# A two-layer encoder trunk on one core: the last stage's gate columns begin behind its first rows, the first group is gated at the end, and convolutions that read PSUM banks go first

## The chip, the cores and the metric

The kernel runs on one core of one Trainium2 chip. The metric is the device time of one execution, in microseconds (us). All arithmetic is float32; a product is made of three matmuls on operands that are split in a high and a low part (below).

## What is computed

The reference, cut to what matters here:

```
sc = silu(c)
for l in (0, 1):
    shift, scale, gate = split(sc @ ada_w[l] + ada_b[l])        # 2048 columns each
    h = rmsnorm(x, g_pre[l]) * (1 + scale) + shift
    if l == 0:                                                   # mLSTM, 8 heads
        proj = h @ a_w_in
        qk = silu(causal_conv(proj[:, :4096], conv_w, conv_b))   # 4 taps along the tokens
        y = mlstm(qk, v, gates) ... @ a_w_out
    else:                                                        # band attention, 16 heads
        k, v = modulate(rmsnorm(x, kv_g)) @ kv_w
        y = (attention(h @ w_q, k, v) * silu(h @ w_z)) @ b_w_out
    x = x + gate * rmsnorm(y, g_post[l])
```

x has 512 tokens of 2048 columns. The last product, `@ b_w_out`, is 512 x 2048 by 2048 x 2048; its result y is multiplied column by column with `gate * g_post` and token by token with the reciprocal root of its mean square.

## The kernel before

All weights stand in DRAM in the order in which they are used (`stream()`), in pieces of up to 128 x 1024 floats. `wpiece` (L188) loads the next piece on SP's queue (L200, tile `wr`), has ScalarE (ACT) round it to its high part (L182, `wh`) and VectorE (DVE) subtract for the low part (L183, `wl`); the two together are `split`. `mm3` then issues three matmuls for each product (L224): hi*hi, hi*lo, lo*hi. Raw pieces have two buffers and a third where a spare pool is named (every third piece), high and low parts have three each, so a piece is split when TensorE (PE) has ended the piece three before it.

The tile framework builds the program: it puts each instruction in its engine's queue in an order that a scheduler sets from program order, priorities (`tc.high_priority(AHEAD)` moves what is in it ahead) and its own estimate of when things are ready; `keep_in_program_order` pins instructions of one kind among themselves. Each engine then works its queue strictly in order, SP's DMA queue too: an instruction that waits holds all that stand behind it. A pool's memory may be reused by a later pool, tile by tile.

The adaLN columns are sums over `sc`: for a block of 128 columns (`mod` column i) two loads of 128 x 1024 floats (`ada_load`, L378) and two DVE reductions (`ada_sum`, L382; a reduction and a short accumulator read each) against a broadcast copy of `sc`. There are 128 blocks; most are done in the background of heads 0 to 3 of the first layer (`background(n)`), the last 16 (blocks 80 to 95, the second layer's gate) in the last stage.

Heads 2 and 3 of the first layer: for each of four 128-column blocks of q and k, `proj_a` (L242) makes a product in a PSUM bank of `psP` (five banks), and `conv` (L526) reads that bank four times: ACT for one tap (L529) and DVE for three (L531), then SiLU and a split. After each, `background(4)` adds four reductions. The value product `ps_v` follows and takes four banks of the same pool.

The last stage (from L1086) works in four groups g of 512 output columns. `proj_b` (L245) goes through the 2048 rows of `b_w_out` two blocks k0, k0 + 1 at a time, each step with one weight piece and, for group 0, one load of two attention output tiles (`y2_tile`, L1100: DRAM `y2c[i]` to `y2r`, then `split` into the stationary tiles `y2`; the first two go to the weight pool, the others share two buffers of the pool `op`). A step is 24 matmuls for four token blocks m; group 3 is done in two halves of two token blocks with 12 matmuls a step. The dictionary `at` names what is called ahead of step k0. `evac` (L784) reads a finished bank: DVE multiplies with the broadcast gate row `gb` (the tile `ssum`) into `yo`, ACT sums the squares. `finish(m)` multiplies with the reciprocal root, adds x and stores.

The gate itself: `gate_sums` sums the up to four pending loads and issues the next four; `gates_out` (L564) multiplies four blocks with `g_post`, turns them to a row with one PE transpose (`ps_gg`), copies it with ACT and writes it to DRAM (`ggd`); `gate_row` (L780) loads the 512 columns of a group back to all partitions. The order is written in `gate_steps`:

```
gate_steps = {
    0: {0: gate_sums, 4: gate_sums, 8: gate_sums, 10: lambda: (gate_part(0), gate_row(1, 0)), 12: gate_sums},
    1: {0: gate_sums, 2: lambda: gate_part(1), 4: gate_sums, 8: gate_sums, 10: lambda: gate_part(2), 12: gate_sums},
    2: {0: gate_sums, 4: lambda: gate_part(3)},
    3: {},
}
```

Of the kernel before, what the change touches and what calls it, by code (L numbers as in the profile page):

```python
# [9 lines left out]
F32 = mybir.dt.float32  # L10
F32R = mybir.dt.float32r
AF = mybir.ActivationFunctionType
ALU = mybir.AluOpType
AX = mybir.AxisListType

P = 128
D = 2048
S = 512
KT = D // P
# [13 lines left out]
AHEAD = 300  # L33
RAW_BUFS = 2

PAIRS = [(0, 1), (2, 3)]
# [9 lines left out]
HALF = 3  # L46
# [78 lines left out]
CW = KVG + 16  # L125
CBIAS = CW + 128
# [6 lines left out]
def hybrid_trunk(ctx, tc, xT, xN, c, adaT, cols, wst, wg, ext, kc, out):  # L133
    nc = tc.nc
# [8 lines left out]
    def pool(name, bufs=1, **kw):  # L143
        return tc.tile_pool(name=name, bufs=bufs, reuse_waits="tile", **kw)
# [7 lines left out]
    csc = dram.tile([1, D], F32, name="csc")  # L152
# [15 lines left out]
    ssum = const.tile([P, S], F32, name="ssum")  # L168
# [7 lines left out]
    def col(i):  # L176
        return cl[:, i : i + 1]
# [3 lines left out]
    def split(hi, lo, src):  # L181
        nc.scalar.copy(hi, src)  # L182
        nc.vector.tensor_tensor(lo, src, hi.bitcast(F32), op=ALU.subtract)  # L183
# [58 lines left out]
    def proj_a(mat, xs, ps, t0=0, t1=S):  # L242
        proj(mat, xs, [ps], 8, 0, len(xs), len(xs) - 1, t0, t1)
# [107 lines left out]
    def newp(name):  # L351
        return psP.tile([P, S], F32, tag="p", name=name)

    def newa(name):
        return psA.tile([P, S], F32, tag="a", name=name)
# [25 lines left out]
    def ada_sum(i, j, at, pin=lambda ins: ins, sc=None):  # L381
        pin(nc.vector.tensor_tensor_reduce(  # L382
            at, at, (sc or scB)[:, j * D // 2 : (j + 1) * D // 2], 1.0, mod[:, i : i + 1] if j else col(CB + i),
            ALU.mult, ALU.add, mod[:, i : i + 1]
        ))
# [25 lines left out]
    for i in range(4):  # L411
        ps = newp(f"ps_c{i}")
# [9 lines left out]
    for q in range(4):  # L422
        pair = []
# [30 lines left out]
    for k0, k1 in BLOCKS:  # L454
# [10 lines left out]
        for i, acc in enumerate(later):  # L465
            ps = newa(f"ps_l{i}_{k0}")
# [56 lines left out]
            nc.tensor.transpose(pt[:, j * 8 : j * 8 + 8], e[:, j * P : (j + 1) * P], ident[:8, :8])  # L523
        nc.vector.tensor_copy(aT.rearrange("p a b -> p (a b)"), pt[:, :32])

    def conv(ps, ch, name):  # L526

        acc = tp.tile([P, S], F32, tag="t", name=f"cv_{name}")
        nc.scalar.activation(acc, ps, AF.Identity, bias=col(CBIAS + ch), scale=col(CW + 96 + ch))  # L529
        for d in range(1, 4):  # L530
            nc.vector.scalar_tensor_tensor(  # L531
                acc[:, d:], ps[:, : S - d], col(CW + 32 * (3 - d) + ch), acc[:, d:], op0=ALU.mult, op1=ALU.add
            )
        nc.scalar.activation(acc, acc, AF.Silu)
        t = hp.tile([P, 2, S], F32R, tag="qk", name=f"qk_{name}", bufs=4)
        split(t[:, 0, :], t[:, 1, :], acc)
        return t
# [12 lines left out]
    def background(n):  # L550

        for a in loaded:
            ada_sum(*a, tc.keep_in_program_order)
        loaded.clear()
        for b, (i, j) in enumerate(pending[:n]):
            p, bufs = (ap_, ADA_BUFS) if b < ADA_BUFS else (bp, 2)
            loaded.append(ada_load(i, j, p, bufs, tc.keep_in_program_order))
        del pending[:n]
# [28 lines left out]
    def pair(c, name, f=HEAD_PAIRS, at={}):  # L587
        z1, z2 = (acp.tile([P, 2, 256], F32, tag="so", name=f"{name}_{i}", bufs=6) for i in range(2))
        proj_s("a_w_in", h1, h1s, f, z1, z2, name, hq, (2, 2), at)
        return [z.rearrange("p a t -> p (a t)") for z in (z1, z2)]  # L590
# [32 lines left out]
    for h in range(NH):  # L623
        for i in (2 * h, 2 * h + 1):
            nc.sync.dma_start(bsc[i], ext[i].partition_broadcast(P))
        chs = [2 * h, 2 * h + 1, 16 + 2 * h, 16 + 2 * h + 1]
        if h == 0:
            so = oz[:4]
        qk = []
        for i in range(4):  # L630
            if h > HALF:
                if i % 2 == 0:
                    zs = pair((i // 2) * (V0 // 2) + h * DK, f"zq{h}_{i}")
                ps = zs[i % 2]
            elif h < 2:
                ps = (lead, qk1)[h][i]
            else:
                ps = newp(f"ps_qk{h}_{i}")
                proj_a("a_w_in", h1, ps)
            qk.append(conv(ps, chs[i], f"{h}_{i}"))  # L640
            if 1 < h <= HALF:
                background(4)
        zs = ps = None
# [45 lines left out]
        for i in range(4):  # L689
            if h >= HALF:  # L690
                f = HEAD_PAIRS if h > HALF else RAMP[i]
# [5 lines left out]
            elif h:  # L697
                ps = newp(f"ps_o{h}_{i}")
# [4 lines left out]
        for i in range(4):  # L703
            if h >= HALF:
                break
            if h:
                ps = newp(f"ps_z{h}_{i}")
                proj_a("a_w_in", h1, ps)
            else:
                ps = oz[4 + i]  # L710
# [12 lines left out]
        for i in range(4):  # L723
            d = slice(i * P, (i + 1) * P)
            ps = newa(f"ps_n{h}_{i}")
# [9 lines left out]
        ps = newa(f"ps_q{h}")  # L735
# [41 lines left out]

    gb = ssum

    def gate_row(layer, g):  # L780

        nc.sync.dma_start(gb, ggd[layer, 4 * g : 4 * g + 4, :].rearrange("k p -> (k p)").partition_broadcast(P))

    def evac(ps, m, g, dst):  # L784
        nc.vector.tensor_tensor(dst, ps, gb, op=ALU.mult)
        nc.scalar.activation(newa(f"sqy{m}_{g}"), ps, AF.Square, accum_out=ssq[:, 4 * m + g : 4 * m + g + 1])

    def row_rstd(m):
# [178 lines left out]
    bias = at.tile([P, S], F32, name="bias")  # L967
# [119 lines left out]
    op = ost.enter_context(pool("op", bufs=KT))  # L1087
    rp = ost.enter_context(pool("x2", bufs=8))
    yo = [[] for _ in range(4)]
# [26 lines left out]
            nc.sync.dma_start(out[m, :, g * S : (g + 1) * S], y)  # L1116

    scC = op.tile([P, D], F32, tag="sc", name="scC", bufs=1)
    nc.sync.dma_start(scC, csc.rearrange("a d -> (a d)").partition_broadcast(P))
    gate_cols = [(80 + i, j) for i in range(KT) for j in range(2)]  # L1120
    gate_in = []

    def gate_sums():

        for a in gate_in:
            ada_sum(*a, tc.keep_in_program_order, scC)
        gate_in[:] = [ada_load(i, j, op, 4, tc.keep_in_program_order) for i, j in gate_cols[:4]]
        del gate_cols[:4]

    def gate_part(g):  # L1130
        gates_out(1, 4 * g, 4 * g + 4, op, bufs=1)

    gate_steps = {
        0: {0: gate_sums, 4: gate_sums, 8: gate_sums, 10: lambda: (gate_part(0), gate_row(1, 0)), 12: gate_sums},
        1: {0: gate_sums, 2: lambda: gate_part(1), 4: gate_sums, 8: gate_sums, 10: lambda: gate_part(2), 12: gate_sums},
        2: {0: gate_sums, 4: lambda: gate_part(3)},
        3: {},
    }
    for g in range(4):
        if g:  # L1140
            spare[0] = op
        for pair in [range(4)] if g < 3 else PAIRS:
            ps = [newp(f"ps_y1_{g}_{m}") for m in pair]
            at = {4: lambda: finish(0), 6: lambda: finish(1)} if pair == PAIRS[1] else {}
            if 0 < g < 3:
                at = {k: lambda k=k: fetch_x(2 * (g - 1) + k // 12) for k in (2, 12)}
            add_at(at, gate_steps[g] if pair != PAIRS[1] else {})
            if g and pair != PAIRS[1]:
                add_at(at, {8: lambda: gate_row(1, g)})
            proj_b("b_w_out", y2_tile, ps, ms=pair, at=at, late=3 if pair == PAIRS[1] else 0)  # L1150
            with tc.high_priority(AHEAD):
                for p, m in zip(ps, pair):
                    yo[m].append(op.tile([P, S], F32, tag="o", name=f"yo{m}_{g}"))
                    evac(p, m, g, yo[m][g])
    finish(2)
    finish(3)
    assert wpos[0] == len(order)
# [56 lines left out]
```

## Time and profile before

| what | value |
|---|---|
| runs, us | 2832.49, 2839.56, 2838.55; median 2838.55 |
| profiled execution | 2837.93 us, of which the span from first to last instruction 2836.2 us |
| mean granted TensorE clock | 0.993 |
| PE busy | 2773.2 us, 98% of the span |
| DVE busy | 2153.3 us, 76% |
| ACT busy | 1372.7 us, 48% |
| last stage, first matmul to end of span | 2614.2 to 2836.2 us |

How to read it: the rows are of one execution. In a timeline row stand the start, the length, the engine, the line, the operation, output and input tiles, and in brackets how long the engine had been idle and what ended that. In a row of the stretches stand the limits, the length, the busy time of each engine with its count of instructions, the granted TensorE clock (1.00 is full speed) and the DMA engines' busy share. SPq is SP's DMA queue.

### The profile page before, as it was taken

To read this page: it belongs to the slowest core of one execution; us is meant where nothing else is said; L and a number is where in the kernel's file an instruction comes from. 1 tells how busy PE (TensorE), PEld (TensorE's weight loads), DVE (VectorE), ACT (ScalarE), POOL (GpSimd) and SP (SyncE) were. 2 spreads that over 40 slices of the span, in tenths; PEclk is the share of its full clock that TensorE was granted. 3 is DMA by queue.
4 is the path that set the end of the run, shared out by engine and by line. 5 is a ranking of instruction groups with operands and counts; after the bars stand their busy time and mean duration, and the time that the engine had idled before them with its cause. 6 is when DMAs were issued, how large, how long until landed. Compare 5 with 4: busy or idle time off the path is not lost.

```text
span 2836.2 us, 42097 instructions
## 1 busy us (share of the span) xinstructions
PE 2773.2 (98%) x15959; PEld 2443.3 (86%) x15959; DVE 2153.3 (76%) x3750; ACT 1372.7 (48%) x2034; POOL 0.2 (0%) x4
## 2 busy tenths in 40 slices
PE   7999999999999999999999999999999999999698
PEld 5787887888998989989898888888998999999587
DVE  7986988889885876858767445568875888988565
ACT  4234534233554554545545445568434566666223
POOL 0000000000000000000000000000000000000000
PEclk9999999999999999999999999999999999999899
DMA  8875797886232332323324657788435444444864
GB/s 293 301 253 176 248 333 263 309 304 247 94 116 90 105 112 86 109 99 103 118 90 162 214 198 235 235 279 279 147 134 197 145 130 127 122 130 138 292 234 170
DMA packets 177813, 526.02 MB, mean 185 GB/s; under 512 B 19093, under 2 KB 37557, under 8 KB 176969
## 3 DMA queue, kind: packets, MB, share of 16 engines
q1 hardware_dynamic: 177610, 523.33, 54.4%
q8 instruction: 125, 2.05, 0.3%
q14 instruction: 78, 0.64, 0.1%
HBM read 489.65 MB, written 38.85 MB: 186 GB/s over the span
## 4 chain that ended last, share of the span: by engine, by line
PE 78%; DVE 9%; DMA 8%; issue 3%; ACT 2%; SPq 0%; DVEq 0%; ACTq 0%
PE ps_y L224 18%; PE ps_v L224 9%; PE ps_azo L224 5%; DMA ada<-in_adaT 4%; PE ps_kv L224 4%; PE ps_az L224 3%; PE ps_bzo L224 3%; PE ps_cz L224 3%; PE ps_dz L224 3%; PE ps_czo L224 3%; PE ps_dzo L224 3%; PE ps_o L224 3%; DVE wl L183 3%; DVE ada L382 2%; DMA wr<-in_wst 2%
## 5 line engine op out<-in xcount | busy, mean ns | idle before, releaser
L182 ACT CAST wh<-wr 128x1024 fp32r<-128x1024 f32 (+3 forms) x586 | 585.7, 1001 | 718.7 <-PE ps_y L224 217.9
L183 DVE TENSOR_TENSOR wl<-wr,wh 128x1024 fp32r<-128x1024 f32 (+3 forms) x586 | 678.4, 1159 | 322.1 <-ACT wh L182 321.1
L224 PE MATMUL ps_y<-wh,y 128*128 128x512 f32 x1536 | 478.7, 392 | 24.1 <-ACT y L182 23.0
L224 PEld LDWEIGHTS ps_y<-wh,y 128*128 128x128 f32 x1536 | 289.4, 189 | 85.2 <-ACT y L182 23.8
L182 ACT CAST wsh<-ws 128x384 fp32r<-128x384 f32 (+1 forms) x261 | 163.3, 626 | 370.0 <-issue 139.1
L224 PE MATMUL ps_v<-wh,h 128*128 128x512 f32 x1024 | 324.6, 393 | 3.5 <-DVE cv L531 3.4
L224 PE MATMUL ps_y<-wl,y 128*128 128x512 f32 x768 | 300.2, 391 | 0.8 <-DVE wl L183 0.8
L183 DVE TENSOR_TENSOR wsl<-ws,wsh 128x384 fp32r<-128x384 f32 (+1 forms) x261 | 181.3, 695 | 120.2 <-ACT wsh L182 118.4
L224 PEld LDWEIGHTS ps_v<-wh,h 128*128 128x128 f32 x1024 | 193.7, 189 | 44.8 <-DVE cv L531 4.2
L224 PE MATMUL ps_v<-wl,h 128*128 128x512 f32 x512 | 200.6, 392 | 0.0
L224 PEld LDWEIGHTS ps_y<-wl,y 128*128 128x128 f32 x768 | 144.9, 189 | 31.3 <-DVE wl L183 1.5
L224 PE MATMUL ps_kv<-wh,hkv 128*128 128x512 f32 x512 | 159.2, 390 | 0.0
L382 DVE CUSTOM_DVE_ANT_0 ada<-ada,scB,cl 128x1024 f32<-128x1024 f32 x112 | 143.2, 1280 | 18.8 <-DMA ada<-in_adaT 18.3
L382 DVE CUSTOM_DVE_ANT_0 ada<-ada,scB,mod 128x1024 f32<-128x1024 f32 x112 | 143.3, 1280 | 17.5 <-DMA ada<-in_adaT 15.7
L207 DVE TENSOR_TENSOR ws<-wr 128x256 f32<-128x256 f32 (+1 forms) x261 | 131.6, 514 | 30.7 <-DMA wr<-in_wst 28.8
L224 PEld LDWEIGHTS ps_v<-wl,h 128*128 128x128 f32 x512 | 96.9, 189 | 19.8 <-issue 0.9
L224 PEld LDWEIGHTS ps_kv<-wh,hkv 128*128 128x128 f32 x512 | 96.1, 188 | 19.7
L224 PE MATMUL ps_azo<-h,wh 128*128 128x256 f32 (+1 forms) x406 | 101.4, 331 | 1.2 <-DVE zo L318 1.2
L224 PE MATMUL ps_l<-h,wh 128*128 128x512 f32 x320 | 99.4, 392 | 0.8 <-ACT oz L469 0.8
L224 PE MATMUL ps_kv<-wl,hkv 128*128 128x512 f32 x256 | 99.8, 390 | 0.3 <-DVE wl L183 0.3
L224 PE MATMUL ps_czo<-h1s,wsh 128*128 128x256 f32 x468 | 89.3, 283 | 0.0
L209 DVE TENSOR_TENSOR ws<-wr 128x128 f32<-128x128 f32 (+1 forms) x261 | 84.7, 334 | 3.4
(383 smaller groups left out, 6214.6 us busy)
## 6 DMA issues: line engine op xcount, KB each, us to landing
wr<-in_wst SPq DMA_DIRECT2D x520, 512.0 KB, 3.9
ada<-in_adaT SPq DMA_DIRECT2D x256, 512.0 KB, 6.7
xt<-nsc SPq DMA_DIRECT2D x48, 256.0 KB, 2.8
yr<-ysc SPq DMA_DIRECT2D x16, 512.0 KB, 3.8
wr<-in_wst SPq DMA_DIRECT2D x30, 256.0 KB, 4.9
wr<-in_wst SPq DMA_DIRECT2D x16, 384.0 KB, 6.3
bsc<-in_ext SPq DMA_DIRECT2D x16, 320.0 KB, 5.9
ysc<-zo SPq DMA_DIRECT2D x20, 256.0 KB, 6.0
```

Source lines behind the costliest of these rows:

```text
L182: nc.scalar.copy(hi, src)
L183: nc.vector.tensor_tensor(lo, src, hi.bitcast(F32), op=ALU.subtract)
L207: nc.vector.tensor_tensor(t[:, : 2 * w], r[:, w : 3 * w], r[:, : 2 * w], op=ALU.subtract)
L209: nc.vector.tensor_tensor(t[:, 2 * w :], r[:, 3 * w :], r[:, w : 2 * w], op=ALU.subtract)
L224: nc.tensor.matmul(ps, a, b, start=start, stop=stop)
L382: pin(nc.vector.tensor_tensor_reduce(at, at, (sc or scB)[:, j * D // 2 : (j + 1) * D // 2], 1.0, mod[:, i : i + 1] if j else col(CB + i), ...
```

## The change

Two things change, both of them in order.

First, `conv` puts its four readings of the PSUM bank in `tc.high_priority(AHEAD)` for heads 2 and 3. The instructions are the same.

Second, the gate of the last stage. The broadcast of `sc` (`scC`) and the first four `ada` loads move from the head of group 0 to its step 10 (`gate_begin`); the blocks are taken in the order 84 to 95, then 80 to 83, so that the gate of group 0 comes last; each group's `gate_part` and `gate_row` shift with them. Group 0 is evacuated by a plain DVE copy in place of the multiplication (the four `evac` of group 0); its gate row goes to a tile of its own, `gb0`, ahead of step 10 of group 3's first half, and four DVE multiplications of 128 x 512 (`gate_first`) at step 14 apply it in place. The number of loads, reductions and matmuls stays; DVE gains the four multiplications, and SP keeps four gate rows.

```
-    def conv(ps, ch, name):
+    def conv(ps, ch, name, first):
         acc = tp.tile([P, S], F32, tag="t", name=f"cv_{name}")
-        nc.scalar.activation(acc, ps, AF.Identity, bias=col(CBIAS + ch), scale=col(CW + 96 + ch))
-        for d in range(1, 4):
-            nc.vector.scalar_tensor_tensor(
-                acc[:, d:], ps[:, : S - d], col(CW + 32 * (3 - d) + ch), acc[:, d:], op0=ALU.mult, op1=ALU.add
-            )
+        with tc.high_priority(AHEAD if first else 0):
+            nc.scalar.activation(acc, ps, AF.Identity, bias=col(CBIAS + ch), scale=col(CW + 96 + ch))
+            for d in range(1, 4):
+                nc.vector.scalar_tensor_tensor(
+                    acc[:, d:], ps[:, : S - d], col(CW + 32 * (3 - d) + ch), acc[:, d:], op0=ALU.mult, op1=ALU.add
+                )
...
-            qk.append(conv(ps, chs[i], f"{h}_{i}"))
+            qk.append(conv(ps, chs[i], f"{h}_{i}", 1 < h <= HALF))
...
-    def evac(ps, m, g, dst):
-        nc.vector.tensor_tensor(dst, ps, gb, op=ALU.mult)
+    def evac(ps, m, g, dst, gated=True):
+        if gated:
+            nc.vector.tensor_tensor(dst, ps, gb, op=ALU.mult)
+        else:
+            nc.vector.tensor_copy(dst, ps)
...
-    nc.sync.dma_start(scC, csc.rearrange("a d -> (a d)").partition_broadcast(P))
-    gate_cols = [(80 + i, j) for i in range(KT) for j in range(2)]
+    gb0 = op.tile([P, S], F32, tag="gb", name="gb0", bufs=1)
+    gate_cols = [(80 + i, j) for i in [*range(4, KT), *range(4)] for j in range(2)]
+    def gate_begin():
+        nc.sync.dma_start(scC, csc.rearrange("a d -> (a d)").partition_broadcast(P))
+        gate_sums()
...
+    def gate_first():
+        for m in range(4):
+            nc.vector.tensor_tensor(yo[m][0], yo[m][0], gb0, op=ALU.mult)
...
     gate_steps = {
-        0: {0: gate_sums, 4: gate_sums, 8: gate_sums, 10: lambda: (gate_part(0), gate_row(1, 0)), 12: gate_sums},
...
+        0: {10: gate_begin, 14: gate_sums},
+        1: {2: gate_sums, 4: lambda: gate_part(1), 6: gate_sums, 10: lambda: gate_row(1, 1), 12: gate_sums},
+        2: {0: lambda: gate_part(2), 2: gate_sums, 6: gate_sums, 8: lambda: gate_part(3), 12: gate_sums},
+        3: {0: gate_sums, 2: lambda: gate_part(0), 10: lambda: gate_row(1, 0, gb0), 14: gate_first},
     }
...
-            if g and pair != PAIRS[1]:
+            if g > 1 and pair != PAIRS[1]:
...
-                    evac(p, m, g, yo[m][g])
+                    evac(p, m, g, yo[m][g], g > 0)
```

What stands in the queues, at the three places of which the prediction speaks. SP's queue before, at the start of the last stage, from the broadcast of `sc` to the first load of attention output that goes to `op` (`y2r2`, the tiles of steps 4 and 5; `ada80_0` is the first half of block 80, `wr552` the weight piece of step 12):

```order
L1119 DMA scC_25580<-csc_76 128x2048
L200 DMA wr552_25865<-in_wst 128x1024
L378 DMA ada80_0_25586<-in_adaT 128x1024
L378 DMA ada80_1_25588<-in_adaT 128x1024
L378 DMA ada81_0_25590<-in_adaT 128x1024
L200 DMA wr555_26013<-in_wst 128x1024
L378 DMA ada81_1_25592<-in_adaT 128x1024
L378 DMA ada82_0_25674<-in_adaT 128x1024
L378 DMA ada82_1_25676<-in_adaT 128x1024
L378 DMA ada83_0_25678<-in_adaT 128x1024
L378 DMA ada83_1_25680<-in_adaT 128x1024
L1104 DMA y2r2_25688<-y2c2_93 128x1024
```

And the same queue of the changed kernel, from the last store of attention output on:

```order
L1054 DMA y2c7_98<-z15_25145 128x512
L200 DMA wr555_25977<-in_wst 128x1024
L1108 DMA y2r2_25668<-y2c2_93 128x1024
L200 DMA wr552_25823<-in_wst 128x1024
L1108 DMA y2r3_25706<-y2c3_94 128x1024
L1128 DMA scC_25580<-csc_76 128x2048
L1108 DMA y2r4_25744<-y2c4_95 128x1024
L378 DMA ada84_0_25777<-in_adaT 128x1024
```

`y2r2` now stands ahead of the broadcast and of all `ada` loads, behind one weight piece.

DVE's queue before, in head 2 of the first layer, around the convolution of its third block (`cv_2_2`, bank `ps_qk2_2`): 128x510 is the second tap on DVE and 128x509 the last.

```order
L531 SCALAR_TENSOR_TENSOR cv_2_2_3724<-ps_qk2_2_3663,cl_99,cv_2_2_3724 128x510
L183 TENSOR_TENSOR qk_2_1_3648<-cv_2_1_3642,qk_2_1_3648 128x512
L382 ISA ada116_0_3573,mod_103<-ada116_0_3573,scB_121,cl_99 128x1024
L382 ISA mod_103 128x1
L183 TENSOR_TENSOR wl108_3913<-wr108_3910,wh108_3912 128x1024
L382 ISA ada116_1_3575,mod_103<-ada116_1_3575,scB_121,mod_103 128x1024
L382 ISA mod_103 128x1
L382 ISA ada117_0_3577,mod_103<-ada117_0_3577,scB_121,cl_99 128x1024
L382 ISA mod_103 128x1
L531 SCALAR_TENSOR_TENSOR cv_2_2_3724<-ps_qk2_2_3663,cl_99,cv_2_2_3724 128x509
```

And of the changed kernel:

```order
L183 TENSOR_TENSOR wl106_3839<-wr106_3836,wh106_3838 128x1024
L532 SCALAR_TENSOR_TENSOR cv_2_2_3724<-ps_qk2_2_3663,cl_99,cv_2_2_3724 128x511
L382 ISA ada113_1_3396,mod_103<-ada113_1_3396,scB_121,mod_103 128x1024
L382 ISA mod_103 128x1
L532 SCALAR_TENSOR_TENSOR cv_2_2_3724<-ps_qk2_2_3663,cl_99,cv_2_2_3724 128x510
L382 ISA ada114_0_3489,mod_103<-ada114_0_3489,scB_121,cl_99 128x1024
L382 ISA mod_103 128x1
L532 SCALAR_TENSOR_TENSOR cv_2_2_3724<-ps_qk2_2_3663,cl_99,cv_2_2_3724 128x509
L183 TENSOR_TENSOR wl107_3883<-wr107_3880,wh107_3882 128x1024
```

The last tap moved from behind the reductions of block 117 and the low part of piece 108 to a place ahead of the low part of piece 107.

DVE's queue of the changed kernel in the first half of group 3, from the gate blocks 80 to 83 on (before, the low parts `wl575` to `wl579` stand there with nothing between them):

```order
L570 TENSOR_TENSOR ggate_105<-mod_103,cl_99 128x4
L183 TENSOR_TENSOR wl575_26662<-wr575_26659,wh575_26661 128x1024
L183 TENSOR_TENSOR wl576_26680<-wr576_26677,wh576_26679 128x1024
L1144 TENSOR_TENSOR yo0_0_25911<-yo0_0_25911,gb0_25581 128x512
L183 TENSOR_TENSOR wl577_26702<-wr577_26699,wh577_26701 128x1024
L1144 TENSOR_TENSOR yo1_0_25915<-yo1_0_25915,gb0_25581 128x512
L1144 TENSOR_TENSOR yo2_0_25919<-yo2_0_25919,gb0_25581 128x512
L183 TENSOR_TENSOR wl578_26730<-wr578_26727,wh578_26729 128x1024
L1144 TENSOR_TENSOR yo3_0_25923<-yo3_0_25923,gb0_25581 128x512
```

Three low parts (`wl577`, `wl578`, and `wl579` right after these rows) now stand behind multiplications that wait for `gb0`.

More of the change, by code (lines that the diff above doesn't have):

```diff
@@ L778, in hybrid_trunk, with gate_row @@
     gb = ssum
-    def gate_row(layer, g):
+    def gate_row(layer, g, gb=ssum):
         nc.sync.dma_start(gb, ggd[layer, 4 * g : 4 * g + 4, :].rearrange("k p -> (k p)").partition_broadcast(P))
-    def evac(ps, m, g, dst):
-        nc.vector.tensor_tensor(dst, ps, gb, op=ALU.mult)
+    def evac(ps, m, g, dst, gated=True):
[3 more added lines that the diff above has]
+            nc.vector.tensor_copy(dst, ps)
         nc.scalar.activation(newa(f"sqy{m}_{g}"), ps, AF.Square, accum_out=ssq[:, 4 * m + g : 4 * m + g + 1])
@@ L1131, in gate_part @@
         gates_out(1, 4 * g, 4 * g + 4, op, bufs=1)
+    def gate_first():
+        for m in range(4):
+            nc.vector.tensor_tensor(yo[m][0], yo[m][0], gb0, op=ALU.mult)
     gate_steps = {
-        0: {0: gate_sums, 4: gate_sums, 8: gate_sums, 10: lambda: (gate_part(0), gate_row(1, 0)), 12: gate_sums},
-        1: {0: gate_sums, 2: lambda: gate_part(1), 4: gate_sums, 8: gate_sums, 10: lambda: gate_part(2), 12: gate_sums},
-        2: {0: gate_sums, 4: lambda: gate_part(3)},
-        3: {},
+        0: {10: gate_begin, 14: gate_sums},
+        1: {2: gate_sums, 4: lambda: gate_part(1), 6: gate_sums, 10: lambda: gate_row(1, 1), 12: gate_sums},
+        2: {0: lambda: gate_part(2), 2: gate_sums, 6: gate_sums, 8: lambda: gate_part(3), 12: gate_sums},
+        3: {0: gate_sums, 2: lambda: gate_part(0), 10: lambda: gate_row(1, 0, gb0), 14: gate_first},
     }
```

## Prediction

> **What bounds the kernel now.** I read the page first, then the stretches of 40 us, the waits of PE, the chain of waits, and last SP's queue at the places that these named. The head of the page, and from the waits the two that the change can reach:
>
> ```profile
> span 2836.2 us, 42097 instructions
> PE 2773.2 (98%) x15959; PEld 2443.3 (86%) x15959; DVE 2153.3 (76%) x3750; ACT 1372.7 (48%) x2034; POOL 0.2 (0%) x4
> ...
> PE ps_y L224 <- ACT y L182: 23.0, 2, 21.5
> PE ps_v L224 <- DVE cv L531: 3.4, 2, 2.9
> ```
>
> PE is busy 98% of the span, and the change adds and removes no matmul. So only time in which PE stands still, or runs at a lower clock, can change. 21.5 us of the 63 idle ones are a single wait in the last stage. The stretches of 40 us (limits, length, busy time of PE, of its weight loads, of DVE, ACT and POOL with counts, granted clock, DMA share, GB/s) show where the clock falls below 1.00 around the two places:
>
> ```profile
> 440.00:480.00 40.00, 37.42 (x165) 30.57 (x163) 35.59 (x50) 17.72 (x21) 0.00 (x0) 1.00 0.76 261
> 480.00:520.00 40.00, 39.70 (x169) 32.95 (x170) 34.52 (x59) 14.19 (x20) 0.00 (x0) 0.92 0.85 295
> ...
> 2640.00:2680.00 40.00, 24.58 (x97) 19.70 (x97) 23.74 (x36) 7.79 (x12) 0.00 (x0) 0.74 0.90 323
> ```
>
> The chain of waits through the second place, and SP's queue there (start, length, line):
>
> ```profile
> 2638.77 8.56 DMA ada<-in_adaT
> 2647.47 1.28 DVE ada L382
> 2649.16 5.56 DMA y2r<-y2c
> ...
> 2631.88 0.33 SPq L1050 DMA_DIRECT2D y2c<-z  x1
> 2632.30 0.38 SPq L1119 DMA_DIRECT2D scC<-csc  x1
> ...
> 2638.11 0.61 SPq L200 DMA_DIRECT2D wr<-in_wst  x1
> 2638.77 10.35 SPq L378 DMA_DIRECT2D ada<-in_adaT  x5
> 2649.16 0.90 SPq L1104 DMA_DIRECT2D y2r<-y2c  x2
> ```
>
> PE waits for the attention output `y2r2`. Its data have been in DRAM since soon after the store at 2631.88, but its load is issued at 2649.16: it stands behind five `ada` loads, which wait 10.35 us for their four buffers, that is for DVE's sums (2647.47), and these for the first `ada` loads to land. It is SP's order that costs the time, not the amount moved.
>
> **The change part by part. The convolution.** PE alone around the stop (limits, length, busy, clock, DMA share, GB/s), and two instructions of DVE, the low part of `wl108` and the tap that ends the stop:
>
> ```profile
> 477.26:480.30 3.04, 0.17 (x2) 0.89 0.77 237
> 480.30:486.43 6.13, 6.13 (x14) 0.50 0.91 319
> 486.68:492.12 5.44, 5.44 (x25) 1.00 0.62 200
> ...
> 475.95 1.22 DVE L183 TENSOR_TENSOR wl<-wr,wh 128x1024 fp32r<-128x1024 f32 x1
> ...
> 479.50 0.74 DVE L531 SCALAR_TENSOR_TENSOR cv<-ps_qk,cl,cv 128x509 f32<-128x509 f32 x1
> ```
>
> `ps_v` needs the bank that the last tap of `cv_2_2` reads at 479.50. PE stands from 477.43 to 480.30, 2.87 us; then 14 matmuls take 6.13 us at clock 0.50, where at full clock (25 in 5.44) they would take 3.05: 3.08 lost. The waits have 0.5 more of the same kind (3.4 less 2.9). Together 6.45. In the changed order this tap stands ahead of `wl107`, which is itself ahead of the row of 475.95; so it is done before 477.43, when PE wants the bank, and the wait goes with its half clock. What is late next is what it passes: low parts of weights and reductions, up to three taps each time. DVE has little room for this in the later stretches:
>
> ```profile
> 680.00:720.00 40.00, 39.55 (x191) 33.24 (x190) 38.53 (x81) 17.83 (x29) 0.00 (x0) 1.00 0.49 171
> 720.00:760.00 40.00, 39.31 (x260) 35.99 (x260) 37.60 (x84) 20.80 (x32) 0.00 (x0) 1.00 0.27 93
> ```
>
> 38.53 of 40 us are full, and PE loses 0.45 + 0.69 us there. The DVE work that isn't done while PE stands must be done somewhere, so I bound what comes back between 0 and all 6.45, and take 1.0, near the 1.14 that such full stretches show. Term: -6.45 + 1.0 = **-5.5**.
>
> **The stall of the last stage.** PE's first matmul with `y2r2`'s tile, the stop ahead of it, the time behind it, and the clock during it:
>
> ```profile
> 2633.73:2655.42 21.69, 0.16 (x2) 0.57 0.93 340
> 2655.42:2660.28 4.86, 4.86 (x12) 0.50 0.87 293
> ...
> 2636.00:2637.00 1.00, 0.00 (x0) 0.00 (x0) 0.23 (x1) 0.00 (x0) 0.00 (x0) 0.93 0.28 115
> ...
> 2655.42 0.79 PE L224 MATMUL ps_y<-wh,y 128*128 128x512 f32 x1 [21.53 <-ACT y L182]
> ```
>
> The loads' times from issue to landing, each kind in the last stage (count, size, median), and those of the gate row with their limits:
>
> ```profile
> wr<-in_wst SPq DMA_DIRECT2D x39, 512.0 KB, 3.3
> ...
> DMA to landing us min/median/max: 3.4/5.2/7.0
> ```
>
> Now the store of `y2c7` at 2631.88 is followed by `wr555` in the slot that `scC` had (2632.30), and `y2r2` follows 0.4 us later, at 2632.7. The landing lies between a weight piece's 3.3 us and its own 5.56 of before, which shared the DMA engines with `ada` loads; I take the middle, 4.4: 2637.1. From landing to PE were 0.70 us (2655.42 - 2649.16 - 5.56): PE goes on at 2637.8. It stopped at 2633.89, so a stall of 3.9 us is left (2.8 to 5.1). Term: 3.9 - 21.5 = **-17.6**.
>
> The clock: before, 12 matmuls behind the stall took 4.86 us for 2.61 at full rate, 2.2 lost. Will it fall in a shorter stop? The row of 2636 to 2637 has 0.93, full until 2636.86, so it fell 3.0 us after PE had stopped; in head 2 (0.89 over 3.04 us, half for the last 0.67) it fell at 479.63, 2.2 us after. 3.9 us are longer than both: I let it fall, at a cost between the 2.2 and the 3.08 of head 2, 2.6. Term: 2.6 - 2.2 = **+0.4**. [...]
>
> **The second stall** of that group:
>
> ```profile
> 2681.25 0.50 PE L224 MATMUL ps_y<-wh,y 128*128 128x512 f32 x1 [1.14 <-ACT wh L182]
> 2682.51 0.50 PE L224 MATMUL ps_y<-wl,y 128*128 128x512 f32 x1 [0.76 <-DVE wl L183]
> 2685.37 0.50 PE L224 MATMUL ps_y<-wh,y 128*128 128x512 f32 x1 [1.43 <-ACT y L182]
> ...
> 2675.79 2.49 DMA ggd<-gg
> 2678.68 6.00 DMA y2r<-y2c
> ```
>
> 1.14 + 0.76 + 1.43 = 3.3 us. The last load of attention output was issued at 2678.68 behind the gate row, which waited for the store `ggd`. In the changed program neither gate row nor `ggd` stands in group 0, and a load waits only for its buffer and the weight pieces ahead of it. Counted on from 2637.8 in steps of 5.44 us, each tile lands ahead of its step; the nearest, the last pair, has its low part about 0.9 us ahead of need (an estimate). Term: **-3.3**, bounded by 0 and by 3.3. The `ada` loads that go from here to groups 1 and 2 (12 in group 1, with 8 weight pieces and four loads of x: 24 x 0.5 MB in 43.5 us, 290 GB/s at most) stay under the 323 that 2640 to 2680 shows, and there no load of attention output is left behind them.
>
> **Group 0 without its gate** costs nothing: a copy of 128x512 out of the same bank stands where the multiplication stood, in the shadow of the next group's matmuls. A copy isn't in the trace in this form; between 0 and the multiplication's 0.69 us, I take the same.
>
> **Group 0's gate in group 3.** The groups of multiplications and of low parts (busy, mean ns), the first half of group 3, and the cadence of its half steps:
>
> ```profile
> L785 DVE TENSOR_TENSOR yo<-ps_y,ssum 128x512 f32<-128x512 f32 x16 | 10.6, 686 | 5.2 <-PE ps_y L224 5.2
> ...
> L183 DVE TENSOR_TENSOR wl<-wr,wh 128x1024 fp32r<-128x1024 f32 x40 | 48.9, 1224 | 55.7 <-ACT wh L182 55.4
> ...
> 2783.00:2805.00 22.00, 22.00 (x99) 18.23 (x98) 11.14 (x11) 9.33 (x11) 0.00 (x0) 1.00 0.52 179
> ...
> 2790.98 1.05 ACT L182 CAST wh<-wr 128x1024 fp32r<-128x1024 f32 x1 [1.67 <-PE ps_y L224]
> 2793.70 1.05 ACT L182 CAST wh<-wr 128x1024 fp32r<-128x1024 f32 x1 [1.67 <-PE ps_y L224]
> ```
>
> Four multiplications are 4 x 0.686 = 2.7 us of DVE, which is busy 11.14 of 22 there: hidden by themselves. But DVE works in order, and `wl577` to `wl579` stand behind them. Count from T, the end of group 2. The last sums and the copy of the transposed row end at about T + 9.9 (four reductions of 1.28 us behind four evacuations), the store takes 2.49, so `gb0` is issued at T + 12.5 and lands at T + 15.9 to 19.5 (3.4 to 7.0; median T + 17.7). `wl577` is needed at T + 19.3 (a half step takes 2.72 us, 2793.70 - 2790.98) and wants 0.68 + 1.22 ahead: a landing by T + 17.3 costs nothing, and each us behind it one. On SP's queue one piece stands between the store and `gb0`, and `wr579`, behind both, waits until T + 12.5; it is wanted at T + 24.7, 12 us for a load of 3.3, so nothing is late there. These times are estimates from the rows. The transpose itself may hold PE 0.2 to 0.5 us. By the median 0.4 (0 to 2.5). Term: **+0.4**.
>
> The sum: -5.5 - 17.6 + 0.4 - 3.3 + 0.4 = -25.6 us; 2837.93 - 25.6 = **2812.3**. The profiled execution lies 0.6 below the median of the runs, so the scale is the same.
>
> **The rivals.**
> 1. The convolution gives its gain back: DVE, 38.5 of 40 us full, brings `wl` later instead, and PE waits there. For it: that fullness; against it: 35.59 and 34.52 of 40 in head 2. -20.1: 2817.8.
> 2. `wr555`, now ahead of `y2r2`, waits for memory that the attention still holds. For it: before, it was issued only at 2638.11; against it: `scC`, from the same released memory, went out at 2632.30. Then `y2r2` goes at 2638.5, PE at 2643.6, 5.8 later: 2818.1.
> 3. The clock stays in the 3.9 us: 2.6 less, 2809.7. [...]
> 4. Slower: `gb0`'s chain blocks DVE in group 3, with `wl577` to `wl579` behind it and PE waiting for each. It outweighs the rest only when `gb0` lands more than 25.6 us behind T + 17.3, and by more than 0.3% at 34 us behind: 2846. The gate row's loads took 7.0 at most, so this needs a store or sum that is itself held, which I don't see in the order.
> 5. The priority does not move the taps: the order shows that it does; no chance.
>
> **How the numbers follow.** Forecast 0.62 (own range 2808 to 2816: the landing's 1.1 us to both sides, the second stall, the give-back); rival 1 0.15; rival 2 0.08; rival 3 0.08; rival 4 0.02; other ways 0.05. About 0.3% (8.5 us) is what a measurement of this kernel can tell from no change. Forecast and rivals 1 to 3 all lie below that, so faster is 0.95 with 0.02 of the others, same 0.03, slower 0.02. Range: with every term at its good end (nothing given back -6.45, stall 2.8 us -18.7, no fall of the clock -2.2, -3.3, 0) it is 2807.3, and the runs of before reach 5.4 below the profiled one, of which a median may keep 3: 2804. With rival 1 or 2, the landing at 5.56 and `gb0` 1.1 later it is 2820, and the runs reach 1.6 above: 2822.
>
> **What would show it.** In the changed profile: no `ps_v <- cv` wait over 0.5 us in head 2 and clock 1.00 from 480 to 520; `y2r2` issued within 1 us of the last store, a stall of 3 to 5 us followed by about 12 matmuls at 0.50; no idle time in the rest of group 0; at group 3's step 14, `wl577` without a wait above 1.5 us. A stall above 6 us, a `wl` wait in heads 2 and 3 that is new, or an idle PE behind `gb0` would make it wrong.

## The result, and the profile after

The changed kernel takes 2814.77 us (median of 6 runs, 2807.89 to 2816.75) against 2837.96 us before (6 runs, 2832.49 to 2845.58). The ratio is 0.9913, 95% interval 0.9896 to 0.9930, so the change made it faster: by about 24.7 us by the ratio, 23.2 between the two medians. The profiled execution took 2815.08 us.

The head of the page of the changed kernel, and from its waits of PE the two that matter (engine and line, what ended the wait; total, times, longest):

```profile
span 2813.3 us, 42110 instructions
PE 2769.0 (98%) x15959; PEld 2442.2 (87%) x15959; DVE 2153.5 (77%) x3754; ACT 1374.1 (49%) x2034; POOL 0.2 (0%) x4
...
PE ps_n L224 <- DVE so L733: 5.2, 1, 5.2
PE ps_y L224 <- ACT y L182: 4.1, 1, 4.1
```

The 23.0 us at `ps_y` are 4.1 now, and the 3.4 at `ps_v` are gone. But there is a new line on top: `ps_n` waits 5.2 us for `so`, where the kernel before had no such wait. The stretches of 40 us (columns as in the prediction) show the same three places:

```profile
480.00:520.00 40.00, 40.00 (x184) 33.48 (x183) 37.41 (x70) 13.86 (x20) 0.00 (x0) 1.00 0.89 316
600.00:640.00 40.00, 34.82 (x157) 29.20 (x155) 32.24 (x47) 12.39 (x16) 0.00 (x0) 0.91 0.67 220
2600.00:2640.00 40.00, 35.43 (x210) 30.37 (x209) 25.82 (x63) 22.31 (x46) 0.00 (x0) 0.96 0.55 179
2640.00:2680.00 40.00, 40.00 (x175) 32.43 (x175) 29.21 (x42) 15.24 (x25) 0.00 (x0) 1.00 0.90 320
```

480 to 520 is full at clock 1.00, 2640 to 2680 too (24.58 us before), and 600 to 640 has lost 5.2 us and part of its clock. The last stage's stall, on SP's queue and in the chain of waits:

```profile
2630.89 0.33 SPq L1054 DMA_DIRECT2D y2c<-z  x1
2631.32 0.37 SPq L200 DMA_DIRECT2D wr<-in_wst  x1
2631.74 0.44 SPq L1108 DMA_DIRECT2D y2r<-y2c  x1
```

```profile
2631.74 4.52 DMA y2r<-y2c
...
2636.29 0.63 ACT y L182
...
2636.96 45.82 PE ps_y L224 x192
```

`y2r2` goes 0.85 us behind the last store, lands 4.52 us later, and from then on PE works through the rest of group 0 without a gap.

The new wait. DVE's queue ahead of the instruction that frees the bank, and the matmul that waited (in brackets the idle time before it and what ended that):

```profile
609.89 1.28 DVE L382 CUSTOM_DVE_ANT_0 ada<-ada,scB,mod 128x1024 f32<-128x1024 f32 x1 [3.25 <-DMA ada<-in_adaT]
...
612.49 0.68 DVE L714 TENSOR_TENSOR so<-so,sz 128x512 f32<-128x512 f32 x1
...
614.29 0.75 DVE L733 SCALAR_TENSOR_TENSOR so<-ps_n,cl,so 128x512 f32<-128x512 f32 x1
...
615.09 3.25 PE L224 MATMUL ps_n<-p,v 128*128 128x512 f32 x9 [5.18 <-DVE so L733]
```

The three banks of `ps_n` are full, and `so` (L733), which frees them, stands in DVE's queue behind a reduction that waits 3.25 us, with DVE idle, for its load of `ada`. In the kernel before, PE came here 8 us later and went through without a wait (the first line is of before, the second of after):

```profile
612.40 7.44 PE L224 MATMUL ps_n<-p,v 128*128 128x512 f32 x44
...
604.33 5.58 PE L224 MATMUL ps_n<-p,v 128*128 128x512 f32 x33
```

To add up where time went between two executions, I take the start of the same matmul in both timelines:

| from, to | before, us | after, us | difference |
|---|---|---|---|
| start to first `ps_v` of head 2 | 471.4 | 469.4 | -2.0 |
| to first `ps_dzo` (head 3) | 241.8 | 241.2 | -0.6 |
| to first matmul of the last product | 1901.0 | 1903.0 | +2.0 |
| to the last matmul | 212.1 | 189.5 | -22.6 |
| to the end of the span | 9.9 | 10.2 | +0.3 |

The first row is not the change's: up to 437 us the queues of all engines are in the same order, and 1.9 of the 2.0 us are there by then. The whole gain of this pair is in the last stage; the stretch with the convolutions gained 0.6 us.

### The profile page after: what moved, and what is told of

The parts are those of the page before. It is cut to its first block, busy times and chain, and to the rows that moved or that the text cites. A ratio compares the mean times of both kernels' runs of the same rounds, so it can differ in the third digit from the quotient of the medians.

```text
span 2813.3 us, 42110 instructions
## 1 busy us (share of the span) xinstructions
PE 2769.0 (98%) x15959; PEld 2442.2 (87%) x15959; DVE 2153.5 (77%) x3754; ACT 1374.1 (49%) x2034; POOL 0.2 (0%) x4
## 4 chain that ended last, share of the span: by engine, by line
PE 84%; DVE 8%; DMA 4%; issue 2%; ACT 1%; SPq 0%; DVEq 0%; ACTq 0%
PE ps_y L224 18%; PE ps_v L224 10%; PE ps_kv L224 5%; PE ps_azo L224 5%; PE ps_az L224 3%; PE ps_cz L224 3%; PE ps_bzo L224 3%; PE ps_dz L224 3%; PE ps_o L224 3%; PE ps_qk L224 3%; PE ps_czo L224 3%; PE ps_dzo L224 3%; DMA ada<-in_adaT 2%; DVE wl L183 2%; PE ps_s L224 2%
```

## The experiments

The theory (A) after the comparison: the last stage's order gives its gain as forecast, and the precedence of the convolution gives nothing, since PE only comes earlier to `ps_n`, where DVE's order and the loads of `ada` hold it. The other theory (B) is the prediction: 5.5 us stay, and the wait at `ps_n` was chance.

**The precedence alone.**

```
+        with tc.high_priority(AHEAD if first else 0):
+            nc.scalar.activation(acc, ps, ...)
+            for d in range(1, 4): ...
```

> The kernel before with the convolution's four readings put first, and nothing else of the change. Theory A (the gain is handed back): the wait of ps_v on the tap in head 2 is gone, PE reaches the end of head 2 about 6 us earlier, and waits there some 5 us at ps_n for the tile so, whose instruction stands in DVE's queue behind reductions that wait for the loads of ada, with a half clock of some 1.7 us behind it; by the products of head 3 it is 0 to 1.5 us ahead of before, and the whole time is 0 to 1.5 us below before (ratio 0.9995 to 1.000). Theory B (the prediction's term): the 5.2 us at ps_n in the changed kernel's profile were chance of one execution, 5.5 us stay, ratio about 0.998. The last stage keeps its stall of 21.5 us by both.

2844.03 us (11 runs) against 2838.83: ratio 1.0015 (1.0005 to 1.0025). Its waits:

```profile
PE ps_y L224 <- ACT y L182: 25.0, 2, 23.3
PE ps_n L224 <- DVE so L733: 4.6, 1, 4.6
```

The wait at `ps_n` is there, that of `ps_v` is not. From `ps_v` of head 2 to `ps_dzo` it takes 241.1 us (241.8 before): theory A. That the whole is slower (some 4 us by the ratio, 5.2 between the medians, clear of the interval) was expected by neither. Its profiled span is 5.8 us longer than the first one of before. 3.3 of them lie between `ps_dzo` and the last product, where the second profile of the kernel before (below) is 1.8 us longer than the first too, and 3.5 in the last stage, where all queues have the order of before. I can't say whether that is more than where the loads happened to land.

**The gate alone.**

```
-            qk.append(conv(ps, chs[i], f"{h}_{i}", 1 < h <= HALF))
+            qk.append(conv(ps, chs[i], f"{h}_{i}", False))
```

> The changed kernel without the precedence of the convolution: only the gate of the last stage is moved. Theory A: the last stage from its first matmul to the last one is 22 to 23 us shorter than before, as in the changed kernel, the whole time within 1.5 us of the changed kernel, ratio to before 0.991 to 0.993; ps_v waits 2.9 us in head 2 again and ps_n does not wait. Theory B: 5.5 us slower than the changed kernel, ratio about 0.993 to 0.995.

2817.33 us, ratio 0.9922 (0.9908 to 0.9935); the intervals of this and of the changed kernel (0.9896 to 0.9930) overlap widely. The last stage takes 191.5 us, 20.6 less than before where 22 to 23 were expected: its stall was a little longer than in the changed kernel (4.7 us against 4.1), and the half clock twice as long (6.83 us against 3.41, from its fall).

```profile
PE ps_y L224 <- ACT y L182: 4.7, 1, 4.7
PE ps_n L224 <- DVE so L733: 3.2, 1, 3.2
PE ps_v L224 <- DVE cv L532: 2.6, 2, 1.9
```

The gate carries the gain. Theory A said that `ps_v` would wait 2.9 us again in head 2 and `ps_n` not at all; the waits were 1.9 and 3.2 us. So the wait at `ps_n` can come without the precedence too.

**The kernel before and the changed one once more**, for the spread of these places.

> The kernel before once more, unchanged, for its profile: how far the waits at the places of this study differ from one execution to the next where nothing is changed. If the 2.87 us of ps_v in head 2, the 21.5 us of the last stage and the absence of a wait at ps_n belong to the program, they come again within 0.5 us. If they hang on when loads happen to land (the two kernels without the precedence showed 1.90 and 1.12 us at ps_v, one of them 3.16 us at ps_n), they come out between 1 and 3 us at ps_v, and PE's lead at the end of head 2 between 0 and 7 us.

> The changed kernel once more, unchanged, for its profile. If the changed kernel pays at ps_n by its order, the wait of ps_n for so is there again (3 to 6 us), there is no wait of ps_v in head 2, and the stall of the last stage is again 3.5 to 5 us; if the 5.2 us were chance, ps_n waits under 1 us in this execution.

Of before, the waits and (PE alone: limits, length, busy, clock, DMA share, GB/s) the stretch behind:

```profile
PE ps_v L224 <- DVE cv L531: 2.3, 2, 1.4
...
480.00:520.00 40.00, 40.00 (x184) 1.00 0.90 319
```

Where the first execution stood 2.87 us and then lost 3.08 at half clock, this one stands 1.44 and the clock stays at 1.00. Over the five executions without the precedence the wait was 2.87, 1.90, 1.12, 1.44 and 1.94 us, and only the first fell to half clock there. The last stage's stall came again within 0.3 us (21.79). Of the changed kernel:

```profile
PE ps_n L224 <- DVE so L733: 3.3, 1, 3.3
```

All five executions with the precedence and the sums in their place waited at `ps_n`: 5.2, 4.6, 3.3, 3.6 and 6.4 us. It belongs to the program; its size does not.

**The sums moved behind `so`.** The last two calls of head 2's background go behind the four readings of `ps_n`. The edit also pins these readings in program order; the move and the pinning were not tried apart.

```
-            nc.vector.tensor_tensor(so[i], so[i], sz, op=ALU.mult)
-            if h:
+            keep(nc.vector.tensor_tensor(so[i], so[i], sz, op=ALU.mult))
+            if h and (h != 2 or i < 2):
                 background(4)
...
-                nc.vector.scalar_tensor_tensor(so[i], ps, ...)
+                keep(nc.vector.scalar_tensor_tensor(so[i], ps, ...))
...
+        if h == 2:
+            background(4)
+            background(4)
         ps = newa(f"ps_q{h}")
```

> The changed kernel with the last two of head 2's calls of the background (eight reductions of ada and eight loads) moved behind the instructions that read ps_n, so that no reduction stands ahead of so there. Theory A (DVE's order at ps_n takes the gain back): the wait of 5.2 us at ps_n and its half clock are gone, and if nothing else is late PE keeps 6 to 8 us at the start of head 3 (2807 to 2809 in all). Rival A2 (the loads of ada through the DMA engines set the pace of this whole stretch, and order in DVE's queue only says where PE pays): the wait comes back in head 3, as a wait of ps_qk or ps_v for a tap, a weight or a bank, and by the end of head 3 PE is again within 1.5 us of the changed kernel. Theory B: no wait at ps_n in either, no difference.

2811.12 us (4 runs), ratio 0.9902 (0.9889 to 0.9916). PE alone, the stretch of `ps_n`:

```profile
600.00:640.00 40.00, 40.00 (x190) 1.00 0.75 267
```

The wait is gone, and from `ps_v` of head 2 to `ps_dzo` it takes 234.6 us in place of 241.2: what head 2 gained stays. Rival A2 of the expectation, that the loads' pace brings the wait back in head 3, fell. In the whole time the gain is smaller, 3.7 us between the medians, and the intervals overlap.

**The sums moved, without the precedence.** The edits of the last one, and the convolution as before.

> The kernel with the sums moved behind so, but without the convolution's precedence: what the precedence is worth once what takes its gain back is gone. Theory A: ps_v waits 1 to 3 us in head 2 and may fall to half clock behind it, nothing waits at ps_n: 2 to 6 us slower than with the precedence (2813 to 2817 us). If the reductions paced by their loads decide it in any case, within 1.5 us.

2815.01 us, ratio 0.9912 (0.9898 to 0.9925): 3.9 us slower than with it in the medians, though the intervals overlap. Its waits of `ps_v` in heads 2 and 3:

```profile
PE ps_v L224 <- DVE cv L532: 3.8, 2, 1.9
```

The stretch from `ps_v` to `ps_dzo` decides more sharply. Over all profiled executions of this study:

| convolution | sums of head 2 | stretch in us, each execution | mean |
|---|---|---|---|
| as before | as before | 241.8, 237.9, 245.1, 236.7 | 240.4 |
| first | as before | 241.2, 237.4, 241.1, 239.3, 245.4 | 240.9 |
| as before | behind `so` | 240.4 | 240.4 |
| first | behind `so` | 234.6, 234.6, 234.3, 236.3 | 235.0 |

In this stretch either edit alone gives nothing, and the two together 5.4 us. That size fits the waits: without the precedence PE stands 1.94 us in head 2 and 1.84 in head 3, and loses 1.7 at half clock behind the second, 5.5 in all. But the third row is one execution, and the first spreads over 8 us. In the whole time the medians with the gate moved are 2817.33 us with neither edit, 2814.77 and 2815.01 with one, 2811.12 with both; their intervals overlap, so the whole time alone would not show it.

**One load ahead.** The kernel before, with `y2r2` alone asked for ahead of the broadcast.

```
+    y2_tile(5)
     nc.sync.dma_start(scC, csc.rearrange("a d -> (a d)").partition_broadcast(P))
```

> The kernel before with one edit in the last stage: y2r2, the attention output of steps 4 and 5, is asked for ahead of the broadcast of sc, so that it stands in SP's queue ahead of it and of all loads of ada; the gate stays where it was, in group 0. If the order of this one load is the whole of the large term, the stall of 21.5 us shrinks to about 4 us (3 to 5) and 17 to 18 us are gained. The second stall of 3.3 us stays or grows (the gate row still waits in group 0, and y2r6 stands behind it): 0 to 8 us more there, since the sums of ada now have less time before the row is wanted. In all 10 to 18 us below before, ratio 0.9935 to 0.9965. If instead the amount of loads in group 0 bounds it, PE waits later in group 0 for most of the 17 us and the ratio is over 0.9965.

2840.37 us (11 runs), ratio 0.9999 (0.9989 to 1.0010): no gain where 10 to 18 us were expected, though its own stall shrank exactly as expected. PE's waits in group 0, and SP's queue between the first two:

```profile
2631.35 0.64 PE L224 MATMUL ps_y<-wh,y 128*128 128x512 f32 x1 [4.05 <-ACT y L182]
2652.40 0.80 PE L224 MATMUL ps_y<-wh,y 128*128 128x512 f32 x1 [13.68 <-ACT y L182]
...
2680.60 0.80 PE L224 MATMUL ps_y<-wh,y 128*128 128x512 f32 x1 [6.16 <-ACT y L182]
```

```profile
2630.53 8.88 SPq L378 DMA_DIRECT2D ada<-in_adaT  x5
...
2644.46 1.05 SPq L1104 DMA_DIRECT2D y2r<-y2c  x2
```

4.05 us at `y2r2`, then 13.68 at `y2r3`, the next tile, which now stands behind the `ada` loads. The stall moved by one tile. The last stage took 215.1 us (212.1 before).

**The first loads of the gate at step 4.** The changed kernel with `gate_begin` at step 4 in place of 10; the sums stay at step 14.

> The changed kernel with the broadcast of sc and the first four loads of ada at step 4 of group 0 in place of step 10; the first sums stay at step 14. So the broadcast and four loads stand ahead of y2r2 in SP's queue again, but no load that waits for a buffer does. If the wait for buffers (DVE's sums) made the stall of 21.5 us, y2r2 is issued about 2.5 us later than in the changed kernel and lands after up to 10 us beside 3 MB of other loads: a stall of 7 to 12 us, and no second wait for y2r3 in group 0 above 2 us. If the bytes ahead make it, the stall is 15 us or more.

One execution, 2825.71 us. The chain of waits, and PE:

```profile
2633.52 0.42 SPq L378
...
2635.64 10.50 DMA y2r<-y2c
```

```profile
2646.83 0.79 PE L224 MATMUL ps_y<-wh,y 128*128 128x512 f32 x1 [16.05 <-ACT y L182]
```

Here no load ahead of `y2r2` waits for a sum, and still the stall is 16.05 us, which I had expected only if the bytes ahead make it. Counted from PE's stop (2630.78 here, 2632.89 in the changed kernel) `y2r2` is issued 6.0 us later, 4.86 behind the stop against 1.15 ahead of it, and its landing takes 10.50 us in place of 4.52: 6.0 + 6.0 make the 12.0 us difference. So, by the difference of single executions, of the 17.5 us that the change took from this stall about 12 came from what stood ahead, half of it in the queue (a weight piece that waits for its buffer until 2633.14 among it) and half in the longer landing, and the remaining 5.5 I put down to the wait for sums.

**The gate of group 0 later in group 3.** `gate_part(0)` at step 6 in place of 2.

> The changed kernel with the transpose and the store of group 0's gate at step 6 of group 3's first half in place of step 2, so that gb0's chain starts later while the multiplications keep their place in DVE's queue. In the changed kernel the transpose follows group 2's end by 9.2 us and gb0 lands 14.7 us behind it. By the working of the prediction a landing costs 1 us per us from 17.3 us behind group 2's end: with the transpose 2.7 to 5.4 us later the landing is at 17.4 to 20.1 us and PE waits 0 to 3 us for the low part wl577. If PE doesn't wait at all though gb0 lands 17.5 us or more behind, the working was wrong.

One execution, 2815.95 us. It tested nothing: the edit left the transpose and the copy at their places in the queues. The load of the gate row, and the first multiplication:

```profile
2771.54 0.33 SPq L783 DMA_DIRECT2D gb<-ggd  x1
...
2774.89 0.69 DVE L1144 TENSOR_TENSOR yo<-yo,gb 128x512 f32<-128x512 f32 x1 [1.03 <-DMA gb<-ggd]
```

`gb0` landed 14.5 us behind group 2's end, as in the changed kernel, and PE did not wait. What a later landing costs stays open.

**Attention output through the weight buffers.** Three kernels on top of the sums moved behind `so`: the first three, four or all eight loads of attention output go to the weight pool's raw buffers, which need no memory of the attention.

```
-... if i < 2 else op.tile([P, 2, S], F32, tag="yr", ...)
+... if i < 3 else op.tile([P, 2, S], F32, tag="yr", ...)
```

> The kernel with the sums moved behind so, and y2r2 loaded to the weight pool's raw buffers like the first two, so that it needs no memory of the attention and stands in SP's queue ahead of the last stores of attention output. The remaining stall of 4.1 us and the half clock behind it (1.5 us) go if the load's late issue is all that keeps PE: 5 to 5.6 us below the kernel with the sums moved, about 2805 to 2806 us, ratio to before about 0.988. If the weight pieces that now come one turn of the raw buffers later, or the next tile (y2r3, still behind the last store), are late next, PE waits 2 to 5 us at ps_y for them: no gain or up to 2 us.

> The kernel with the sums moved behind so, and the first four loads of attention output (y2r0 to y2r3) in the weight pool's raw buffers. In the kernel with three, PE waited for y2r3, whose load was issued behind the last store; here it stands ahead of it. If that late issue is all that is left, both waits of group 0 go and PE gains 5 to 7 us over the kernel with two (about 2805 us, ratio to before 0.988). If the weight pieces that come later (two turns of the raw buffers) or y2r4, now the first behind the last store, are late next, PE waits 3 to 7 us for them: ratio 0.990 to 0.992.

> The same with all eight loads of attention output in the raw buffers, which leaves the attention's memory free for the broadcast of sc and the buffers of ada: their loads now stand ahead of the last stores and between the loads of attention output. The raw buffers then take two loads for each step of group 0, so PE waits for a weight piece or a tile at every step where the sum of a load (3.3 us) and its splitting is not done in 5.4 us: I expect waits of 1 to 3 us at several steps, in all 5 to 15 us more than with two, ratio 0.992 to 0.996. If loads in the raw buffers cost nothing, the waits of group 0 vanish and the ratio is 0.988.

Three: 2811.92 us, ratio 0.9907 (0.9893 to 0.9921). Four: 2815.64 us, 0.9915 (0.9901 to 0.9928). Neither gains: a later tile waits. The load that decides, in the chain of the kernel with three and of that with four:

```profile
2629.94 6.25 DMA y2r<-y2c
```

```profile
2650.22 6.08 DMA y2r<-y2c
```

With three it is `y2r3`, and PE waits 4.71 and then 2.53 us. With four it is not `y2r4`, which the expectation named, but `y2r5`. SP's queue and ACT's splitting of the tiles in the kernel with four:

```profile
2634.34 0.42 SPq L1113 DMA_DIRECT2D y2r<-y2c  x1
2634.81 0.43 SPq L1133 DMA_DIRECT2D scC<-csc  x1
...
2649.85 0.33 SPq L200 DMA_DIRECT2D wr<-in_wst  x1
2650.22 0.91 SPq L1113 DMA_DIRECT2D y2r<-y2c  x2
...
2640.82 1.14 ACT L182 CAST y<-y2r 128x512 fp32r<-128x512 f32 x2 [3.15 <-DMA y2r<-y2c]
2656.32 2.42 ACT L182 CAST y<-y2r 128x512 fp32r<-128x512 f32 x4 [7.75 <-DMA y2r<-y2c]
```

`y2r4` goes at 2634.34 and is split at 2640.82, before PE stops at 2647.48. The next load, `y2r5`, stands behind the broadcast, four `ada` loads and three weight pieces that go out a step apart, the last at 2649.85; it is split at 2656.32, and PE waits 9.5 us. All eight: 2803.49 us (4 runs), ratio 0.9874 (0.9861 to 0.9888), the best of this study, against my expectation of a loss. The two stretches, all engines, and the broadcast of `sc` on SP's queue:

```profile
2600.00:2640.00 40.00, 39.53 (x216) 33.59 (x215) 25.79 (x57) 23.35 (x44) 0.00 (x0) 1.00 0.85 298
2640.00:2680.00 40.00, 40.00 (x179) 32.99 (x178) 32.06 (x46) 12.32 (x20) 0.00 (x0) 1.00 0.90 319
...
2605.77 0.42 SPq L1133 DMA_DIRECT2D scC<-csc  x1
```

No wait of PE for attention output is left, and the last stage takes 183.0 us; with the sums moved alone it took 190.1, with a stall of 4.09 us and some 2.6 lost at half clock. The DMA engines, 0.55 busy from 2600 to 2640 in the changed kernel, are 0.85 busy here: the broadcast goes out at 2605.77 (2636.11 in the changed kernel) and four `ada` loads by 2621, while the attention still runs, so less is left to fetch behind it. That the scheduler can place them there because the other loads no longer take the memory is my reading; it was not tried by itself.

## Why the prediction came out as it did

**The sum was right, by an error on each side.** 2812.3 us was forecast and 2814.77 measured, within the range, and rival 1's price (2817.8) is nearly as near. That the number came so close is luck: in the pair of profiles the convolution's term fell short by 4.9 us, and the last stage gave 2.5 us more than its terms. By its steps:

The stall of the last stage: right, nearly to the tenth. 3.9 us forecast, 4.07 and 4.24 measured; landing 4.4 forecast, 4.52 measured; 0.70 us from landing to PE in both. The second stall (-3.3) is gone as forecast. The gate row in group 3 was given +0.4 and cost nothing: its load was issued 11.1 us behind the end of group 2 and not 12.5, and landed at 14.7, ahead of the forecast's 15.9 to 19.5. In all the last stage gave 22.6 us (22.1 between the second profiles) where the terms made 20.1. Rivals 2 to 4 did not come: the weight piece ahead of `y2r2` went out 0.4 us behind the store, the clock did fall, and `gb0` held nothing up.

Of the cause, the prediction said that SP's order costs the time, "not the amount moved". That is half of it. The two edits beside it show that moving one load up is worth nothing to the whole, and that four loads and the broadcast ahead of `y2r2`, none of them waiting for a sum, already make a stall of 16 us; half of what they add is a longer landing (10.50 us against 4.52), which I read as sharing the DMA engines: they were 0.93 busy over the 10.50 us and 0.89 over the 4.52, at 340 and 291 GB/s. No run tried this by itself. In the changed kernel the first `ada` load goes out behind `y2r4`. The kernel with all eight raw loads gets there the other way: its first four `ada` loads are issued by 2621, while the attention still runs.

The clock: that it would fall in the short stop was right, its price was not. I took +0.4; by stretches of 0.25 us the half clock ended 5.3 us behind the restart before and 3.1 us behind it after, 2.7 and 1.5 us lost, so -1.1. These count only what lies behind the restart. From its fall on, the half clock lasted 23.89 us before and 3.41 us after, and in head 2 before 6.83 us. Rival 3 let the clock stay in a stop of 3.9 us, which no run shows for this place: in the last stage the clock fell in all eight stops of 4.05 to 4.71 us at `y2r2` or `y2r3`. A stop of 3.30 us elsewhere passed without a fall, as the last section shows.

**The step that failed is the convolution's -5.5.** Two things were wrong in it. Its size came from one execution, in which the place was dearer than in four others (2.87 us and a half clock, against 1.12 to 1.94 us and, in those, no half clock); without the chance of that execution 1 to 2 us of this wait were there to gain. And what comes back was sized at 1.0 from full stretches of DVE, while all but 0.6 us came back in this pair, and by the means of the table all of it (0.5 us slower). Rival 1 had the amount right and the mechanism wrong. It is not that DVE was too full: DVE was idle 3.25 us with `so` behind a reduction in its queue. I had asked what the taps are moved past; I had not asked what PE meets next when it comes 6 us earlier, and none of the signs that I named would have caught a wait at `ps_n`.

What stays open: why the precedence alone was some 4 us slower by the ratio though its stretch was not, how much of the variation of 236.7 to 245.4 us in that stretch comes from where loads land, and whether moving the sums alone gives anything, which rests on one profile.

## What to carry to other kernels

When a wait is removed, go on along the engine that is now early, to the next place where it meets an in-order queue, and look for an instruction there that waits for a DMA: two edits that each measured as nothing in their stretch were worth 5.4 us there together. The stall behind SP's queue went on to the next tile when only one load was moved up (4.05 us at `y2r2`, then 13.68 at `y2r3`); count all the tiles of that stage. And before a term is sized from one execution, ask whether the wait hangs on when a load lands: a second profile of the unchanged kernel showed 2.3 us of these waits and no half clock, where the term had 6.45.

## What the runs showed of the hardware

How long the half clock lasted varied from stop to stop. From the granted clock in short stretches around each stop of PE (the third column counts from PE's stop):

| kernel | PE stood, us | clock fell after, us | half clock lasted, us |
|---|---|---|---|
| after, last stage | 4.07 | 3.72 | 3.41 |
| sums behind `so`, last stage | 4.09 | 2.54 | 6.83 |
| after again, last stage | 4.24 | 2.65 | 6.83 |
| before, head 2 | 2.87 | 2.20 | 6.83 |
| after, `ps_n` | 5.18 | 2.59 | 6.83 |
| four raw loads, group 0 | 9.51 | 4.84 | 10.24 |
| one load ahead, second stop | 13.68 | 3.08 | 13.65 |
| before, last stage | 21.53 | 2.97 | 23.89 |

Two of the rows behind the first line (PE alone; clock third from the end):

```profile
2636.50:2637.00 0.50, 0.04 (x1) 0.61 0.63 213
...
2640.00:2640.50 0.50, 0.50 (x3) 0.98 1.04 442
```

In these eight rows the half clock lasted 1, 2, 3, 4 or 7 times 3.41 us, to within 0.03 us, while PE's own stops were 2.87 to 21.53 us long. In the kernel with one load ahead the clock fell at 2631.56, 2641.80 and 2675.94, so 10.24 and 34.14 us apart, 3 and 10 times the same 3.41. Stops of nearly the same length cost differently: 4.07 us in the changed kernel was followed by 1.5 us lost, 4.09 us with the sums behind `so` by about 2.6 (half of what PE worked at half clock), so one execution does not give the price of such a stop. Short stops differ too. The clock fell after one of 2.87 us (head 2 before) and after one of 1.84 us (a `ps_v` of the kernel with the sums moved and no precedence, half clock for 3.41 us); it stayed at 1.00 through one of 1.94 us in that same execution and one of 3.30 us (after again, at `ps_n`). What decides this the runs do not show.

A load of 512 KB took 4.52 us from issue to landing behind one weight piece (the changed kernel), 6.25 behind two (three raw loads) and 10.50 behind the broadcast, a weight piece and four loads of its own size (first loads at step 4). So with more loads ahead the landing was longer here, and not only the place in the queue later; each figure is of one execution, and what went out behind these loads may differ too.
